# Two tiles for the fold of the row maxima, one mask instead of two, and norm weights in shared tiles, in a hybrid attention block on one core

## The chip, the cores and the metric

One core of a Trainium2 chip runs the whole kernel. The metric is the device time of one execution in microseconds, lower is better; a kernel's time is the median of its runs. Engines are named as in the profile: PE is TensorE (PEld its weight loads), DVE is VectorE, ACT is ScalarE, POOL is GpSimd, SP is the sync engine that issues most DMAs.

## What is computed

One decoder layer over 2048 tokens of width 1024: RMSNorm, one input projection, three mixers side by side (latent attention with 8 heads, differential attention with 4 heads of two softmax maps, cross-attention of 4 heads to 256 memory tokens), a SiLU gate and an output projection on top of the residual.

```
h = rms_norm(x, norm_g)
cq, ckv, kr, dq, dk, dv, mq, z = split(h @ w_in)
y_mla  = mla_branch(cq, ckv, kr, positions, ...)
y_diff = diff_branch(dq, dk, dv, positions, ...)
y_mem  = mem_branch(mq, mem, ...)
y = concat(y_mla, y_diff, y_mem) * silu(z)
x = x + y @ w_out
...
# in a causal branch, per block of queries:
sc = where(causal_mask, (q @ k.T) * scale, -1e30)
p  = softmax(sc)
```

## The kernel before

The work is cut into steps: 4 steps m (memory attention), 8 steps d (differential attention, 2 groups of 2 heads), 16 steps a (latent attention, 4 groups of 2 heads); in each group b = 0 to 3 counts blocks of 512 queries. Values are kept as a 16-bit part and a low remainder, so most products are three matmuls (L187 to L189 the projections, L917 to L919 the scores of a step a, L958 to L960 the output).

Softmax needs a bound on each query's row of scores. The kernel estimates it ahead: est_block (L387 to L421) multiplies the 16-bit parts of queries and keys (L398), adds the causal mask on the diagonal by a second matmul into the same PSUM tile (L400), and takes the maximum. For b = 0 VectorE takes it straight from PSUM (L402). For b of 1 to 3 (`fold`) ScalarE copies the first 512 keys of two query tiles into the halves of a tile er (L404), copies each later 512 into a tile ec (L407), VectorE takes the maximum into er (L408), folds er three times (L412) and reduces the last 64 columns (L413):

```
394  er = wk.tile([P, 2, 512], BF16, tag="er", name="er", bufs=1)
404  A.activation(er[:, t % 2], ps, AF.Copy)
408  V.tensor_tensor(er[:, t % 2, 0:n], er[:, t % 2, 0:n], ec[:, 0:n], ALU.max)
412  V.tensor_tensor(er[:, :, 0:n], er[:, :, 0:n], er[:, :, n:2 * n], ALU.max)
413  V.reduce_max(mx[:, m, t - 1:t + 1, 0], er[:, :, 0:64], axis=AX.X)
```

The estimate goes into a column of the query tile (L421), which is transposed again by a DMA on SP (L474 and L484 in a step d, L891 and then L900 in a step a) into a tile qB. Only then can the scores of that head start: L572 in a step d, L917 in a step a. The mask on the diagonal of the scores is a matmul with a second mask tile (mask_t, L575 and L921). ScalarE takes the exponential (L506), VectorE its low remainder (L507), TensorE multiplies by the values (L516, L518, L536).

Pools and names that the change touches: er has one tile and ec four; PSUM has three tiles for estimates (ps_e), two for scores, two for projections. In pool sm, ss (sums of squares, L440 and L624) and rstd (L92, inverse roots, by GpSimd at L97 and L101) have two tiles each. rtab is one tile for the rope tables of a step (L328, GpSimd L332 to L335). The norm weights g_mk and g_mq (L208 to L210, used once, at L242), g_q, g_k and g_n (L304 to L307) have tiles of their own; lamw (L312) is a scratch tile for the lambda.

The order of the work: a planner of costs and due times (steps, fills, Task) only sets the order in which code is recorded and its priorities. From these a scheduler then lays out every engine's instructions once, before the run, by what it believes durations and buffers to be. On the chip each engine goes through its list in that order and waits at semaphores.

Of the kernel before, what the change touches and what calls it, by code (L numbers as in the profile page):

```python
# [11 lines left out]
F32 = mybir.dt.float32  # L12
F16 = mybir.dt.float16
BF16 = mybir.dt.bfloat16
I32 = mybir.dt.int32
AF = mybir.ActivationFunctionType
ALU = mybir.AluOpType
AX = mybir.AxisListType

P = 128  # L20
# [6 lines left out]
NEG = -1.0e30  # L27
# [13 lines left out]
def hybrid_block(ctx: ExitStack, tc: tile.TileContext, x, mem, positions, norm_g, w_in, mla_q_norm_g,  # L41
                 mla_kv_norm_g, w_uq, w_ukv, mla_qn_g, mla_kn_g, diff_qn_g, diff_kn_g, diff_lambda,
                 diff_subln_g, mem_norm_g, w_mem_kv, mem_qn_g, mem_kn_g, w_out, out):
    nc = tc.nc
# [20 lines left out]
    ident = cst.tile([P, P], BF16, name="ident")  # L65
    make_identity(nc, ident)
    mask_t = cst.tile([P, P], BF16, name="mask_t")
    make_lower_triangular(nc, mask_t, val=NEG, diag=False)
    mask_e = cst.tile([P, P], BF16, name="mask_e")
    make_causal_mask(nc, mask_e, mask_val=NEG)  # L70
    mhalf = cst.tile([P, 1], F32, name="mhalf")
# [11 lines left out]
    def gain_row(src, n, name):  # L83
        t = cst.tile([P, n], F32, name=name)
        SP.dma_start(t, src.broadcast_to([P, n]))
        return t
# [4 lines left out]
    def rstd_of(ss, shape, name, tag="rstd", eps=EPS):  # L91
        r = sm.tile([P, 32 if tag == "rstd" else 8], F32, tag=tag, name=name)  # L92
        n = int(np.prod(shape))
        rv = r[:, 0:n]
        if len(shape) == 2:
            rv = rv.rearrange("p (a b) -> p a b", b=shape[1])
        G.tensor_scalar(rv, ss, eps, None, ALU.add)  # L97
        m = mhalf
        if len(shape) == 2:
            m = m.unsqueeze(2)  # L100
        G.tensor_tensor(rv, rv, m.broadcast_to([P] + list(shape)), ALU.pow)  # L101
        return rv
# [99 lines left out]
    def tmp4(name):  # L202
        return wk.tile([P, 1024], F32, tag="t4", name=name, bufs=2)
# [3 lines left out]
    tc.cur_priority = top + 1000  # L207
    g_mk = gain_row(mem_kn_g, 64, "g_mk")  # L208
    g_mq = gain_row(mem_qn_g, 64, "g_mq")
    V.tensor_tensor(g_mk, g_mk, g_mq, ALU.mult)  # L210
    mk = []
# [91 lines left out]
    g_dk = gain_row(diff_kn_g, 32, "g_dk")  # L303
    g_q = gain_row(mla_qn_g, 96, "g_q")  # L304
    g_k = gain_row(mla_kn_g, 96, "g_k")
    g_n = cst.tile([P, 64], F32, name="g_n")
    V.tensor_tensor(g_n, g_q[:, 0:64], g_k[:, 0:64], ALU.mult)  # L307
    g_wo = cst.tile([P, 1], F32, name="g_wo")
    for i in range(2):
        SP.dma_start(g_wo[64 * i:64 * i + 64, :], diff_subln_g[0].rearrange("(p o) -> p o", o=1))  # L310
    V.tensor_scalar_mul(g_wo, g_wo, (1.0 - LAM_INIT) * WS)
    lamw = tmp4("lamw")  # L312
    lamt = lamw[:, 0:128].rearrange("p (a b) -> p a b", b=32)
    SP.dma_start(lamt.rearrange("p a b -> p (a b)"), diff_lambda.rearrange("o a b -> o (a b)").broadcast_to([P, 128]))
# [72 lines left out]
    def est_block(st, i, nmap, mcol, lhs, rhs):  # L387
# [3 lines left out]
        for m in range(nmap):  # L391
            for t in range(4):
                if fold and t % 2 == 0:
                    er = wk.tile([P, 2, 512], BF16, tag="er", name="er", bufs=1)
                for c in range(b + 1):
# [3 lines left out]
                    if c == b:  # L399
                        T.matmul(ps[:, t * P:n], lhsT=ident, rhs=mask_e, start=False, stop=True)  # L400
                    if not fold:
# [22 lines left out]
    def prep_d(st, units):  # L424
# [14 lines left out]
        yield 1.0  # L439
        ss = sm.tile([P, 32], F32, tag="ss", name=f"ss_{nm}")  # L440
        V.reduce_sum(ss, sq.rearrange("p (a d) -> p a d", d=32), axis=AX.X)
# [167 lines left out]
    def prep_m(st, units):  # L609
# [13 lines left out]
        yield 1.0  # L623
        ss = sm.tile([P, 32], F32, tag="ss", name=f"ss_{nm}")  # L624
        V.reduce_sum(ss[:, 0:16], sq.rearrange("p t (m d) -> p (t m) d", d=64), axis=AX.X)
# [93 lines left out]
    def kv_latents():  # L719
        units = []  # L720
        yield from load_w(w_in, [(256, 160)], gx, "lk", units)
        for b in range(NB):
# [11 lines left out]
            r = rstd_of(ss, [4], f"rlk{b}", "rstd_l")  # L734
            tb = rope_tabs(b, g_k[:, 64:96], f"kr{b}")
            kr = cst.tile([P, 4, 32], F32, name=f"krot{b}")
# [87 lines left out]
    def prep_a(st):  # L824
        g, b, nm = st.g, st.b, st.name
        tb = rope_tabs(b, g_q[:, 64:96], nm)
        q = new_qkv(f"qkv_{nm}")[:, :, 0:192].rearrange("p t (h d) -> p t h d", d=96)
# [436 lines left out]
```

## Time and profile before

| | |
|---|---|
| time, median of 3 runs | 1371.22 us (1367.65 to 1371.38) |
| the profiled execution's own time | 1372.15 us |
| its span, first to last instruction | 1370.3 us |
| mean granted TensorE clock | 0.989 |
| PE, DVE, ACT, POOL busy | 94%, 82%, 66%, 24% of the span |

A row of a group of instructions gives the source line, the engine, the operation, out<-in with shapes, the count, then busy time in us and the mean of one in ns, then the time the engine stood idle just before them and what ended it. Durations come from the profiled execution. A busy PE is counted by modelled ends of pipelined matmuls, so its idle time is a lower bound.

### The profile page before, as it was taken

How to read it: one execution, taken by the hardware profiler on the slowest of the kernel's cores; microseconds unless marked ns; L12 is line 12 of the kernel's file. 1: busy time of each engine (PE TensorE's matmuls, PEld its weight loads, DVE VectorE, ACT ScalarE, POOL GpSimd, SP SyncE). 2: the span in 40 equal slices, each digit the busy share in tenths (PEclk: the TensorE clock that was granted, in tenths of full speed). 3: DMA queues.
4: the chain of work that ended last, by engine and by line, in shares of the span. 5: the costliest groups of instructions: out<-in, count | busy, mean ns of one | idle time of the engine just before them, and what ended most of it. 6: DMA issues, size and time to landing. Idle time of an engine off the chain costs nothing.

```text
span 1370.3 us, 35041 instructions
## 1 busy us (share of the span) xinstructions
PE 1293.0 (94%) x13616; PEld 829.5 (61%) x13616; DVE 1123.1 (82%) x2713; ACT 903.9 (66%) x2163; POOL 333.9 (24%) x477
## 2 busy tenths in 40 slices
PE   5988999999999999999998999999999998999998
PEld 2434556667667767667775656666655665655554
DVE  4657888879889867889899889999998998886745
ACT  6656544677878646786896667677766877665521
POOL 2322232403042133113202143223243323200000
PEclk9999999999999999999999999999999999999999
DMA  7998844223113322447446166347525643275452
GB/s 231 199 208 184 184 111 101 59 60 88 41 25 71 79 34 60 78 110 193 124 98 144 40 167 150 84 107 167 109 71 118 145 99 55 40 155 158 141 184 70
DMA packets 294262, 155.52 MB, mean 113 GB/s; under 512 B 239952, under 2 KB 272848, under 8 KB 294096
## 3 DMA queue, kind: packets, MB, share of 16 engines
q1 hardware_dynamic: 294064, 153.29, 47.7%
q8 instruction: 106, 1.74, 0.5%
q14 instruction: 60, 0.49, 0.1%
q0 software_dynamic: 32, 0.00, 0.0%
HBM read 61.75 MB, written 34.34 MB: 70 GB/s over the span
## 4 chain that ended last, share of the span: by engine, by line
PE 56%; DVE 13%; POOL 9%; ACT 8%; DMA 8%; issue 4%; SPq 1%; ACTq 0%; DVEq 0%; POOLq 0%
PE pp L189 6%; PE pp L187 6%; PE pp L188 6%; PE pe L398 5%; DVE plo L507 4%; PE pv L518 3%; PE pv L516 3%; PE pv L536 3%; PE st L572 3%; PE pp L958 3%; PE pp L959 3%; PE pp L960 3%; PE st L917 3%; PE st L918 2%; PE st L919 2%
## 5 line engine op out<-in xcount | busy, mean ns | idle before, releaser
L506 ACT ACTIVATE p<-st 128x512 f32<-128x512 f32 (+3 forms) x672 | 356.2, 551 | 167.2 <-PE st L919 65.8
L507 DVE TENSOR_TENSOR plo<-p 128x512 f16<-128x512 f32 (+3 forms) x672 | 404.6, 615 | 63.1 <-ACT p L506 59.2
L407 ACT ACTIVATE ec<-pe 128x512 bf16<-128x512 f32 (+3 forms) x384 | 197.2, 536 | 39.2 <-PE pe L400 17.1
L516 PEld LDWEIGHTS <-p 128*128 128x128 bf16 x2304 | 186.0, 99 | 51.5 <-DVE y_a L924 4.7
L518 PEld LDWEIGHTS <-p 128*128 128x128 bf16 x2304 | 173.1, 98 | 39.4 <-issue 4.1
L408 DVE TENSOR_TENSOR er<-er,ec 128x512 bf16<-128x512 bf16 (+3 forms) x384 | 141.5, 378 | 29.9 <-ACT ec L407 15.2
L404 ACT ACTIVATE er<-pe 128x512 bf16<-128x512 f32 x192 | 110.0, 606 | 47.2 <-DVE mx_a L413 18.1
L536 PEld LDWEIGHTS <-plo 128*128 128x128 f16 x2304 | 123.1, 97 | 23.7 <-DVE plo L507 5.8
L917 PE MATMUL st<-qB_a,kT_a 97*128 97x512 f16 (+1 forms) x320 | 112.8, 353 | 13.6 <-ACT p L506 8.7
L516 PE MATMUL pv<-V_d,p 128*128 128x65 f16 x1088 | 116.8, 194 | 3.3 <-DVE y_d L579 2.9
L189 PEld LDWEIGHTS <-ht_x 128*128 128x128 f16 x896 | 87.7, 98 | 52.9 <-ACT ht_x L137 3.9
L188 PEld LDWEIGHTS <-ht_x 128*128 128x128 f16 x896 | 87.8, 98 | 47.8 <-issue 4.0
L518 PE MATMUL pv<-V_d,p 128*128 128x64 f16 x1088 | 116.5, 196 | 0.0
L572 PE MATMUL st<-qB_d,kT_d 97*128 97x512 f16 (+1 forms) x320 | 111.4, 353 | 5.2 <-ACT zc L704 2.1
L187 PEld LDWEIGHTS <-ht_x 128*128 128x128 f16 x896 | 87.7, 98 | 47.1 <-issue 2.8
L516 PE MATMUL pv<-V_a,p 128*128 128x65 f16 x1088 | 112.6, 193 | 2.0 <-DVE y_a L924 1.9
L918 PE MATMUL st<-qB_a,kT_a 96*128 96x512 f16 (+1 forms) x320 | 112.6, 352 | 0.0
L398 PE MATMUL pe<-kT_d,qB_d 96*128 96x512 f16 (+2 forms) x320 | 106.2, 348 | 6.8 <-ACT ec L407 3.6
L518 PE MATMUL pv<-V_a,p 128*128 128x64 f16 x1088 | 112.2, 195 | 0.0
L919 PE MATMUL st<-qB_a,kT_a 96*128 96x512 f16 (+1 forms) x320 | 111.9, 350 | 0.0
L398 PE MATMUL pe<-kT_a,qB_a 96*128 96x512 f16 (+2 forms) x320 | 100.0, 349 | 7.7 <-DMA qB_a<-qs_a 4.6
L189 PE MATMUL pp<-w_d,ht_x 128*128 128x512 f16 x256 | 97.0, 379 | 0.0
(293 smaller groups left out, 3337.7 us busy)
## 6 DMA issues: line engine op xcount, KB each, us to landing
xt_x<-in_x_dram SPq DMA_DIRECT2D x16, 512.0 KB, 4.7
xr<-in_x_dram SPq DMA_DIRECT2D x16, 512.0 KB, 3.6
part<-xr SPq DMA_DIRECT2D x16, 512.0 KB, 2.9
ysc<-yt SPq DMA_DIRECT2D x31, 256.0 KB, 2.3
yl<-ysc SPq DMA_DIRECT2D x15, 512.0 KB, 4.6
zsc<-zc SPq DMA_DIRECT2D x48, 128.0 KB, 2.1
xa<-part SPq DMA_DIRECT2D x12, 512.0 KB, 3.6
out_dram<-xa SPq DMA_DIRECT2D x12, 512.0 KB, 2.9
```

The source lines that it names most:

```text
L187: T.matmul(ps[:, :n], lhsT=ht[:, 0, k], rhs=wt[:, 0, :n], start=(k == 0), stop=False)
L188: T.matmul(ps[:, :n], lhsT=ht[:, 0, k], rhs=wt[:, 1, :n], start=False, stop=False)
L189: T.matmul(ps[:, :n], lhsT=ht[:, 1, k], rhs=wt[:, 0, :n], start=False, stop=(k == NK - 1))
L398: T.matmul(ps[:, 0:n], lhsT=lhs(m, t), rhs=rhs(m, c, n // P), start=True, stop=c < b)
L407: A.activation(ec[:, 0:n], ps[:, 0:n], AF.Copy)
L506: A.activation(p32[:, :n], ps[:, :n], AF.Exp, scale=self.scale)
L507: V.tensor_tensor(plo[:, :n], p32[:, :n], phi[:, :n], ALU.subtract)
L516: T.matmul(pvv[:, t, 0:65], lhsT=phi[:, c], rhs=vt[:, 0:65], start=(j == 0 and t == 0), stop=False, skip_group_check=True)
L518: T.matmul(pvv[:, t, 0:64], lhsT=phi[:, c], rhs=vt[:, 65:129], start=False, stop=False, skip_group_check=True)
L536: last["pv"] = T.matmul(pvv[:, t, 0:65], lhsT=plo[:, c], rhs=vt[:, 0:65], start=False, stop=(j == self.njt - 1), skip_group_check=True)
L572: T.matmul(ps[:, :n], lhsT=st.kTs[j // 4][0:97, h, j % 4, m % 2, :], rhs=st.qB[h][0:97, t0:4, m % 2, :], start=True, stop=not diag)
L917: T.matmul(ps[:, :n], lhsT=kt[0:97, h, j % 4, 0, :], rhs=q[0:97, 0, t0:4, :], start=True, stop=False)
```

## The change

The fold gets two er tiles. To make room, the mask of the estimates, mask_e, goes away: the matmul that added it as ident^T times mask_e now takes mask_t as the stationary operand and ident as the moving one, which is mask_t transposed. The tiles ss and rstd get one buffer. g_mk and g_mq become the halves of a tile under the tag rtab. g_q and g_k shrink to the 32 rope columns; g_n is loaded by itself and multiplied by weights that are loaded into lamw. That makes two small DMAs on SP more and two set-up instructions on GpSimd fewer; all other engines have as many instructions as before.

```diff
-    mask_e = cst.tile([P, P], BF16, name="mask_e")
-    make_causal_mask(nc, mask_e, mask_val=NEG)
...
-        r = sm.tile([P, 32 if tag == "rstd" else 8], F32, tag=tag, name=name)
+        r = sm.tile([P, 32 if tag == "rstd" else 8], F32, tag=tag, name=name, bufs=1 if tag == "rstd" else 2)
...
-    g_mk = gain_row(mem_kn_g, 64, "g_mk")
-    g_mq = gain_row(mem_qn_g, 64, "g_mq")
-    V.tensor_tensor(g_mk, g_mk, g_mq, ALU.mult)
+    g_m2 = wk.tile([P, 2, 64], F32, tag="rtab", name="g_m2", bufs=1)
+    SP.dma_start(g_m2[:, 0], mem_kn_g.broadcast_to([P, 64]))
+    SP.dma_start(g_m2[:, 1], mem_qn_g.broadcast_to([P, 64]))
+    g_mk = g_m2[:, 0]
+    V.tensor_tensor(g_mk, g_mk, g_m2[:, 1], ALU.mult)
...
-    g_q = gain_row(mla_qn_g, 96, "g_q")
-    g_k = gain_row(mla_kn_g, 96, "g_k")
-    g_n = cst.tile([P, 64], F32, name="g_n")
-    V.tensor_tensor(g_n, g_q[:, 0:64], g_k[:, 0:64], ALU.mult)
+    g_q = gain_row(mla_qn_g[:, 64:96], 32, "g_q")
+    g_k = gain_row(mla_kn_g[:, 64:96], 32, "g_k")
+    g_n = gain_row(mla_qn_g[:, 0:64], 64, "g_n")
...
+    SP.dma_start(lamw[:, 192:256], mla_kn_g[:, 0:64].broadcast_to([P, 64]))
+    V.tensor_tensor(g_n, g_n, lamw[:, 192:256], ALU.mult)
...
-                    er = wk.tile([P, 2, 512], BF16, tag="er", name="er", bufs=1)
+                    er = wk.tile([P, 2, 512], BF16, tag="er", name="er", bufs=2)
...
-                        T.matmul(ps[:, t * P:n], lhsT=ident, rhs=mask_e, start=False, stop=True)
+                        T.matmul(ps[:, t * P:n], lhsT=mask_t, rhs=ident, start=False, stop=True)
...
-        ss = sm.tile([P, 32], F32, tag="ss", name=f"ss_{nm}")
+        ss = sm.tile([P, 32], F32, tag="ss", name=f"ss_{nm}", bufs=1)
```

The scheduler lays out all engines anew. Three places show how. In the rows, numbers tell tiles of one name apart; numbers of the change are lower by 4 for the same tile, and source lines move by 1 or 2 (L404 of before is L405 of the change, L917 is L918, L196 is L194).

VectorE, in the first estimate of a step d with b = 1. Before:

```order
L408 TENSOR_TENSOR er_2542<-er_2542,ec_2558 128x256
L583 SCALAR_TENSOR_TENSOR y_d00_2868<-pv_3110,rl_3164,y_d00_2868 128x64 x4
L412 TENSOR_TENSOR er_2542<-er_2542 128x2x256
L412 TENSOR_TENSOR er_2542<-er_2542 128x2x128
L412 TENSOR_TENSOR er_2542<-er_2542 128x2x64
L413 TENSOR_REDUCE mx0_d01_2541<-er_2542 128x2
L507 TENSOR_TENSOR plo_3177<-p32_3176 128x256
L507 TENSOR_TENSOR plo_3206<-p32_3205 128x128
L705 SCALAR_TENSOR_TENSOR zc002_3019<-zc002_3019,pp_2994 128x256
L408 TENSOR_TENSOR er_2565<-er_2565,ec_2598 128x384
```

After the change:

```order
L409 TENSOR_TENSOR er_2538<-er_2538,ec_2554 128x256
L584 SCALAR_TENSOR_TENSOR y_d00_2864<-pv_3106,rl_3160,y_d00_2864 128x64 x4
L413 TENSOR_TENSOR er_2538<-er_2538 128x2x256
L409 TENSOR_TENSOR er_2561<-er_2561,ec_2594 128x384
L413 TENSOR_TENSOR er_2538<-er_2538 128x2x128
L413 TENSOR_TENSOR er_2538<-er_2538 128x2x64
L414 TENSOR_REDUCE mx0_d01_2537<-er_2538 128x2
```

The first maximum into the second tile moved from behind the reduction of the first tile to between its folds.

ScalarE, in the estimate of step d03 (er_5238 before, er_5234 after, the same tile). Before:

```order
L196 ACTIVATE kl0_6589<-pp_6704 128x160
L726 ACTIVATE lsk0_6750<-kl0_6589 128x4x128
L727 ACTIVATE lsk0_6750<-kl0_6589 128x4x32
L506 ACTIVATE p32_6085<-st_6083 128x512
L404 ACTIVATE er_5238<-pe_5239 128x512
L404 ACTIVATE er_5238<-pe_5306 128x512
L407 ACTIVATE ec_5331<-pe_5329 128x512
```

After the change:

```order
L408 ACTIVATE ec_5227<-pe_5224 128x256
L405 ACTIVATE er_5234<-pe_5235 128x512
L434 ACTIVATE qkv_d10_5805<-pp_6256 128x256
L370 ACTIVATE V_d10_5806<-pp_6256 128x2x64
L507 ACTIVATE p32_5676<-st_5674 128x512
L439 ACTIVATE sq_d10_6395<-qkv_d10_5805 128x1024
L408 ACTIVATE ec_5257<-pe_5255 128x512
L375 ACTIVATE zt_d10_5807<-pp_6256 128x128
L507 ACTIVATE p32_5725<-st_5723 128x512
L408 ACTIVATE ec_5262<-pe_5260 128x512
```

The first copy into that tile moved ahead of the last projection of step d10 (qkv_d10, V_d10, sq_d10) and of all of the latents (kl0, lsk0), which it used to follow.

TensorE, in the estimates of head 1 of step a31 (qB1_a31), from the first of its eight L398 on. Before:

```order
L398 MATMUL pe_21267<-kT_a30_20656,qB1_a31_21194 128x512
L917 LDWEIGHTS kT_a21_18622
L917 MATMUL st_20961<-qB1_a23_19747,kT_a21_18622 128x512
L918 LDWEIGHTS kT_a21_18622
L918 MATMUL st_20961<-qB1_a23_19747,kT_a21_18622 128x512
```

After the change:

```order
L399 MATMUL pe_21263<-kT_a30_20652,qB1_a31_21190 128x512
L399 LDWEIGHTS qB1_a31_21190
L399 MATMUL pe_21266<-kT_a31_21149,qB1_a31_21190 128x128
L401 LDWEIGHTS mask_t_89
L401 MATMUL pe_21266<-ident_84,mask_t_89 128x128
L399 LDWEIGHTS qB1_a31_21190
L399 MATMUL pe_21272<-kT_a30_20652,qB1_a31_21190 128x512
L537 LDWEIGHTS plo_20802
```

The first estimate was followed by scores of another head, and the second stood 130 rows further; now the first three follow each other, and the eight lie within 60 rows instead of 448.

## Rows read from the trace of the kernel before

**Rows 1.** The page, busy us, share of the span and instructions of each engine.

```profile
PE 1293.0 (94%) x13616; PEld 829.5 (61%) x13616; DVE 1123.1 (82%) x2713; ACT 903.9 (66%) x2163; POOL 333.9 (24%) x477
```

**Rows 2.** Windows: stretch, its us, busy PE, PEld, DVE, ACT, POOL, clock, DMA.

```profile
200.00:1000.00 800.00, 775.94 (x8879) 534.66 (x8877) 696.07 (x1790) 572.18 (x1462) 209.04 (x275) 0.99 0.41 95
1000.00:1200.00 200.00, 182.69 (x2163) 119.53 (x2162) 182.47 (x439) 144.10 (x351) 70.86 (x91) 0.97 0.41 88
411.90:415.30 3.40, 2.96 (x46) 2.57 (x46) 3.35 (x12) 3.40 (x15) 0.56 (x2) 0.50 0.09 18
...
1176.50:1183.30 6.80, 6.37 (x29) 2.74 (x29) 5.43 (x10) 3.26 (x7) 6.52 (x8) 0.50 0.32 61
```

**Rows 3.** Waits of PE: waiter <- waited for: us in total, times, longest.

```profile
PE st L917 <- ACT p L506: 8.7, 13, 2.5
...
PE pe L398 <- ACT ec L407: 4.5, 8, 1.5
PE st L917 <- DMA qB_a<-qs_a: 4.3, 4, 1.5
...
PE pe L398 <- ACT er L404: 3.5, 6, 1.4
```

**Rows 4.** Waits of ACT.

```profile
ACT er L404 <- DVE mx_a L413: 18.1, 16, 3.7
...
ACT er L404 <- DVE mx_d L413: 15.1, 15, 3.1
...
ACT ec L407 <- DVE er L408: 7.0, 7, 2.6
```

**Rows 5.** Groups of instructions by line, ACT.

```profile
L407 ACT ACTIVATE ec<-pe 128x512 bf16<-128x512 f32 (+3 forms) x384 | 197.2, 536 | 39.2 <-PE pe L400 17.1 <-PE pe L398 10.9 <-DVE er L408 7.0
...
L404 ACT ACTIVATE er<-pe 128x512 bf16<-128x512 f32 x192 | 110.0, 606 | 47.2 <-DVE mx_a L413 18.1 <-DVE mx_d L413 15.1 <-PE pe L398 11.4
```

**Rows 6.** Timeline around 409 us (start, us, engine, instruction, idle before).

```profile
408.69 1.09 ACT L404 ACTIVATE er<-pe 128x512 bf16<-128x512 f32 x2 [3.15 <-DVE mx_d L413]
...
408.38 0.27 DVE L413 TENSOR_REDUCE mx_d<-er 128x2 f32<-128x128 bf16 x1
...
409.33 0.38 PE L398 MATMUL pe<-kT_d,qB_d 96*128 96x512 f16 x1 [1.43 <-ACT er L404]
```

**Rows 7.** Timeline of PE, the four scores that waited for a transpose.

```profile
1130.27 0.38 PE L917 MATMUL st<-qB_a,kT_a 97*128 97x512 f16 x1 [1.31 <-DMA qB_a<-qs_a]
...
1153.39 0.38 PE L917 MATMUL st<-qB_a,kT_a 97*128 97x512 f16 x1 [0.48 <-DMA qB_a<-qs_a]
...
1176.93 0.58 PE L917 MATMUL st<-qB_a,kT_a 97*128 97x512 f16 x1 [1.10 <-DMA qB_a<-qs_a]
...
1214.03 0.39 PE L917 MATMUL st<-qB_a,kT_a 97*128 97x512 f16 x1 [1.45 <-DMA qB_a<-qs_a]
```

**Rows 8.** Timeline of the start: SP, then ACT, then PE.

```profile
15.10 0.33 SPq L85 DMA_DIRECT2D g_q<-in_mla_qn_g_dram  x1
16.40 0.33 SPq L85 DMA_DIRECT2D g_k<-in_mla_kn_g_dram  x1
...
21.70 0.43 SPq L120 DMA_DIRECT2D xt_x<-in_x_dram  x1
...
27.22 1.06 ACT L143 ACTIVATE xh_x<-xt_x 128x1024 f16<-128x1024 f32 x1 [0.57 <-DMA xt_x<-in_x_dram]
...
32.49 0.38 PE L134 MATMUL pt<-ident,xl_x 128*128 128x128 bf16 x4 [2.65 <-DVE ht_x L137]
```

**Rows 9.** Lines L242 and L332 (count, ns, first and last start), and timeline of r_d.

```profile
L242 DVE TENSOR_TENSOR mem_kn<-mem_kn,g_mk x1: 684/684/684, 67.6 to 67.6; 128x512 f32<-128x512 f32 x1
...
L332 POOL TENSOR_TENSOR rt_d<-cos_t,g_dk x8: 318/404/4525, 127.0 to 546.6; 128x64 f32<-128x64 f32 x8
...
269.36 0.68 DVE L457 TENSOR_TENSOR qkv_d<-qkv_d,r_d 128x512 f32<-128x512 f32 x1
...
314.98 0.30 POOL L97 TENSOR_SCALAR r_d<-ss_d 128x32 f32<-128x32 f32 x1 [29.90 <-DVE ss_d L441]
```

More of the change, by code (lines that the diff above doesn't have):

```diff
@@ L8 @@
 from concourse import mybir
-from concourse.masks import make_causal_mask, make_identity, make_lower_triangular
+from concourse.masks import make_identity, make_lower_triangular
 from concourse._compat import with_exitstack
@@ L623, in prep_m @@
         yield 1.0
-        ss = sm.tile([P, 32], F32, tag="ss", name=f"ss_{nm}")
+        ss = sm.tile([P, 32], F32, tag="ss", name=f"ss_{nm}", bufs=1)
         V.reduce_sum(ss[:, 0:16], sq.rearrange("p t (m d) -> p (t m) d", d=64), axis=AX.X)
@@ L734, in kv_latents @@
             r = rstd_of(ss, [4], f"rlk{b}", "rstd_l")
-            tb = rope_tabs(b, g_k[:, 64:96], f"kr{b}")
+            tb = rope_tabs(b, g_k, f"kr{b}")
             kr = cst.tile([P, 4, 32], F32, name=f"krot{b}")
@@ L825, in prep_a @@
         g, b, nm = st.g, st.b, st.name
-        tb = rope_tabs(b, g_q[:, 64:96], nm)
+        tb = rope_tabs(b, g_q, nm)
         q = new_qkv(f"qkv_{nm}")[:, :, 0:192].rearrange("p t (h d) -> p t h d", d=96)
```

## The prediction, made before the changed kernel was run

> **What bounds the kernel now.** I read the busy shares first, then stretches, then the waits of TensorE and ScalarE, then the instructions around the longest of these waits. In the busy shares TensorE stands at 94%, VectorE at 82%, ScalarE at 66% [rows 1]. The stretches show that this is no even mix: from 200 to 1000 us TensorE is idle for 24 us of 800, but from 1000 to 1200 us for 17 of 200, and there VectorE is busy for as long as TensorE, 182.5 against 182.7 us [rows 2]. All matmuls stay, so what can be won is TensorE's idle time, 1370.3 - 1293.0 = 77 us, and what a lowered clock costs after it.
>
> Who ends that idle time is in the waits of TensorE [rows 3]. The scores wait for an exponential (8.7 us) or for a transposed query tile (4.3 us); the estimate of the row maxima (L398) waits for ScalarE to empty a PSUM buffer into er (3.5 us) or ec (4.5 us). ScalarE, for its part, stood still before its copies into er until the last VectorE instruction of the fold before, L413: 18.1 + 15.1 = 33.2 us in 31 waits [rows 4]. That is the single er tile: the 192 copies (606 ns each) fill 96 tiles [rows 5], and each new tile needs the old one folded. The longest of these cases shows the mechanism: VectorE gets to L413 at 408.38, ScalarE had been idle for 3.15 us when it starts er at 408.69, and TensorE, idle for 1.43 us, starts the next estimate at 409.33 [rows 6]. Directly after, from 411.9 to 415.3, the granted clock is 0.50, the lower of its two levels (1.2 and 2.4 GHz); the same stands from 1176.5 to 1183.3 [rows 2].
>
> **The change part by part.**
>
> *Second er tile, direct part.* The copy into er now waits for the fold two tiles back. TensorE's 3.5 us behind er should go. Of the 4.5 us behind ec I take half, 2.2, since such an ec follows an er in ScalarE's queue. Term: -5.7 us; bounds 0 (VectorE is late in any case, and ec, four tiles, stops ScalarE next) and -8.0 (both rows). That the other 25 of the 33.2 us were worth anything I don't assume: TensorE had other matmuls.
>
> *Estimates that stand earlier.* The compiler laid all engines out anew. The four waits of scores for the second transpose of their query tile (1.31, 0.48, 1.10 and 1.45 us, together 4.3) [rows 7] belong, counted along the order, to head 1 of step a22, both heads of a23 and head 1 of a31. Between the last estimate and the first scores of that head stood 354, 212, 294 and 370 rows of TensorE's order; now 516, 588, 668 and 848. The transpose itself is as long as it was, but it starts that much sooner. Term: -4.3 us; bounds 0 (the transposes queue on SP behind others) and -4.3.
>
> *The clock.* Half of TensorE's busy time at the lower level is lost: in 411.9 to 415.3 it is 2.96 / 2, in 1176.5 to 1183.3 it is 6.37 / 2 [rows 2], together 4.7 us. The first follows an er wait [rows 6], the second the transpose wait that ends at 1176.93 [rows 7]. Term: -4.7 us; bounds 0 and -4.7.
>
> *Packing.* This is what the new order costs. The eight estimate matmuls of head 1 of a31 stood within 448 rows of TensorE's order and now stand within 60. Each must be emptied by ScalarE (536 to 606 ns [rows 5]) and folded by VectorE, and TensorE has three PSUM buffers to run ahead with; what it is stopped at, everything behind it is stopped at too. No row shows this. The nearest one is the wait of ec for VectorE's maximum, 7.0 us in 7 cases [rows 4]: it is what ScalarE loses where VectorE can't keep up, and with denser estimates more of it reaches TensorE. Bounds: 0 (other matmuls lie between) and +12 (below, second rival). I take the row, +7.0 us.
>
> *Start.* The weights now take two more loads on SP ahead of the fourth row tile of x, since g_n, g_q and g_k load their own parts and the other half of g_n's product comes through lamw. Loads of this kind follow each other at 15.10 and 16.40; the tile of x is issued at 21.70, ScalarE waits for it until 27.22, and in VectorE's order the copies that TensorE's wait of 2.65 us ends with (32.49) stand behind that tile's low part [rows 8]. Two issues of 0.33 us are the least, two spacings of 1.30 the most: +0.7 to +2.6; ScalarE's slack is spent, so I take +1.5.
>
> *What costs nothing.* The mask matmul keeps shape and count; only which of two 128x128 tiles is loaded and which one streams changes. Two set-up instructions leave GpSimd before anything waits for it. g_m2 in the tile of the rope tables is read for the last time at 67.6 and first written by a table at 127.0 [rows 9]: 59 us of cover, without which GpSimd would wait. One tile each for ss and rstd: r_d of one step is read for the last time at 269.36, and the next step writes it at 314.98 [rows 9]; the cover is the distance between steps, and if it were gone, each of the 28 preparations (4 m, 8 d, 16 a) could stop GpSimd.
>
> **The sum** against the profiled execution (1372.15 us): -5.7 - 4.3 - 4.7 + 7.0 + 1.5 = -6.2, so 1366.0. That execution stands 0.93 us above the median of the runs (1371.22), so 1365.0 on the median's scale. A measurement of this kernel can tell about 0.3%, 4.1 us, from no change: below 1367.1 is faster, above 1375.3 slower.
>
> **The rivals.**
>
> *VectorE sets the pace: no change, 1371.* For it: between 1000 and 1200 us it is as busy as TensorE [rows 2], and the er waits end with VectorE's fold, which runs no faster. A second tile then only moves ScalarE's wait from er to ec and to the exponentials. Against it: VectorE is idle for 18% of the whole span [rows 1]. The terms from er and the clock then shrink to about -1.5, the transposes' stays, packing takes it back: -1.5 - 4.3 + 4.0 + 1.5, about 1371. The Trainium skill, Perfetto Trace Analysis, section Identifying the Most-Contended Engine, would have one work on the engine of highest occupancy and judge TensorE by its weight loads instead of its matmuls. By that rule VectorE (82%) comes before TensorE (weight loads 61%), and a change that takes no instruction off VectorE brings nothing. The rows agree in part, between 1000 and 1200 us alone.
>
> *Packed estimates stop TensorE: slower, 1379.* The place is L398 in the d and a steps, 36 blocks with a fold (12 in d, 24 in a). One wait for ec cost TensorE 4.5 / 8 = 0.56 us [rows 3]. If one such wait comes per block, that is 20 us where 8.0 stood: +12. Without term one: 1372.15 + 12 - 4.3 - 4.7 + 1.5 = 1376.7; two more stretches at the lower clock (2.96 / 2 each) make it 1379.6, or 1379 on the median's scale. It decides from the point at which waits of L398 for er and ec together grow by more than the 7.5 us that transposes, clock and start bring. For it: the order is made with no knowledge of the chip's delays, and VectorE has little to spare late in the span. Against it: until 1000 us TensorE is nearly never starved with the same estimates, and the second er lets VectorE lag by one more tile.
>
> *The exponentials profit too: 1355.* ScalarE's 33.2 us of standing still are in one queue with the exponentials. If half of the 8.7 us of scores that wait for them [rows 3] goes with two more stretches at the lower clock (3.0 us) and packing costs only 4: -5.7 - 4.3 - 4.7 - 4.4 - 3.0 + 4.0 + 1.5 = -16.6, or 1355. Against it: around most of those waits ScalarE was busy with projections and stacks, not waiting for er.
>
> That the change doesn't do what it says can be left out: VectorE's order shows a maximum of the next tile ahead of the last folds of the one before.
>
> **How the numbers follow.** Forecast (1365, own range 1358 to 1369) 0.45; no change 0.23; slower 0.20; larger gain 0.12. Of the forecast's 0.45 about 0.07 lies above 1367.1. Faster: 0.38 + 0.12 = 0.50. Same: 0.07 + 0.21 = 0.28. Slower: 0.20 + 0.02 = 0.22. The range goes from 1353, below which some 0.05 of the larger gain lies, to 1380, above which lies half of the slower case.
>
> **What would show it.** Right: the waits of er for L413 fall from 33 us to under 10; L917 no longer waits for qB_a at the four places; no lowered clock near 412 and 1177; TensorE idle for some 76 us (77 - 5.7 - 4.3 + 7.0 + 1.5). Packing at its price: L398's waits for ec and er together are 8 to 10 us, mostly ec. Wrong: those waits at 16 or more (slower), er's wait replaced by one of equal size for ec (no change), or new gaps of TensorE that no step here names, since the whole order was laid out anew.

## The result and the profile after

The changed kernel takes 1379.46 us (median of 5 runs, 1376.52 to 1382.19), the kernel before beside it 1371.34 (5 runs, 1367.65 to 1373.46): a ratio of 1.0054, with a 95% interval of 1.0031 to 1.0077. It is slower by 0.5%, where the forecast was 1365, a gain. The profiled execution takes 1379.46 us, with a span of 1377.7 against 1370.3. Lines after L70 stand a few lines off: L398 is now L399, L404 L405, L407 L408, L413 L414, L506 L507, L917 L918; in the kernels of the experiments they are a few lines off again (L396 to L404 for L398).

The page's busy times of the changed kernel, to be read beside [rows 1]:

```profile
PE 1295.7 (94%) x13616; PEld 830.6 (60%) x13616; DVE 1109.4 (81%) x2713; ACT 901.3 (65%) x2163; POOL 346.8 (25%) x475
```

TensorE is busy for 2.7 us more with the same instructions and idle for 82.0 instead of 77.3 us (the prediction had 76). Who ends its idle time, first two rows of the kernel before that [rows 3] leaves out:

```profile
PE pe L398 <- DMA qB_a<-qs_a: 4.6, 3, 2.0
...
PE pe L398 <- DMA qB_d<-s_d: 0.5, 1, 0.5
```

then the changed kernel:

```profile
PE st L918 <- ACT p L507: 12.8, 17, 2.5
PE pe L399 <- DMA qB_a<-qs_a: 9.4, 5, 3.1
...
PE pt L132 <- DVE ht_x L135: 4.6, 1, 4.6
...
PE pe L399 <- ACT er L405: 3.6, 3, 2.1
...
PE pe L399 <- ACT ec L408: 3.2, 7, 0.8
PE pe L399 <- DMA qB_d<-s_d: 2.5, 2, 1.8
```

and ScalarE's before er:

```profile
ACT er L405 <- DVE mx_d L414: 4.9, 3, 2.7
...
ACT er L405 <- DVE mx_a L414: 3.1, 4, 1.7
```

What the change was to do, it did: er waits for the fold for 8.0 instead of 33.2 us [rows 4], and the row of scores waiting for qB_a [rows 3, 7] is gone. But the estimates' waits for er and ec fell only from 8.0 to 6.8 us, the scores' waits for an exponential rose from 8.7 to 12.8, and two rows have grown that no step of the prediction names: the estimates wait longer for the *first* transpose of their own query tile, 9.4 us in the a steps (5 cases, 4.6 in 3 before) and 2.5 in the d steps (0.5 before). The two longest on TensorE's timeline:

```profile
747.00 0.72 PE L399 MATMUL pe<-kT_a,qB_a 96*128 96x512 f16 x2 [2.54 <-DMA qB_a<-qs_a]
...
807.26 0.66 PE L399 MATMUL pe<-kT_a,qB_a 96*128 96x512 f16 x3 [3.12 <-DMA qB_a<-qs_a]
```

One trace of each would not be enough for this, since a wait differs from trace to trace. But all three kernels with the changed order (the changed one, and after_no_loads and gn_on_gpsimd below) lie outside the six that have the order of before, but for a few places (the kernel before, and mask_only, sums_single, norms_before_order, two_loads and two_er_before_order below):

| TensorE's waits, us | order of before | changed order |
|---|---|---|
| scores of a steps for an exponential | 6.4 to 8.7 | 11.8 to 12.8 |
| estimates for the first transpose, a steps | 2.7 to 5.7 | 9.4 to 11.7 |
| estimates for the first transpose, d steps | 0.5 to 2.2 | 2.5 to 3.6 |
| estimates for er and ec | 8.0 to 11.2 | 6.6 to 7.1 |

The start lost more than the two issues on SP. On the timelines of VectorE, ScalarE, SP and TensorE:

```profile
26.63 0.23 DVE L313 TENSOR_TENSOR g_n<-g_n,lamw 128x64 f32<-128x64 f32 x1 [1.77 <-DMA lamw<-in_mla_kn_g_dram]
...
28.78 0.20 ACT L321 ACTIVATE lams<-lams 128x2 f32<-128x2 f32 x1 [2.75 <-DVE lams L320]
29.75 1.06 ACT L141 ACTIVATE xh_x<-xt_x 128x1024 f16<-128x1024 f32 x1 [0.77 <-DMA xt_x<-in_x_dram]
...
22.82 0.43 SPq L118 DMA_DIRECT2D xt_x<-in_x_dram  x1
...
35.02 0.58 PE L132 MATMUL pt<-ident,xl_x 128*128 128x128 bf16 x4 [4.62 <-DVE ht_x L135]
```

SP issues the fourth tile of x 1.1 us later than before [rows 8], but ScalarE takes it up 2.5 us later, and what it waits for last is this tile's own transfer (0.77 us): from the issue to ScalarE's start are 6.9 us, where it was 5.5 (21.70 to 27.22). In the traces of the experiments (but for the two with a late set-up) that tile takes 5.3 to 6.7 us to land without the two further loads and 6.9 to 7.4 with them; what makes it longer isn't shown. The exponential of lambda (L321), which stands ahead of it and waits for VectorE and its late small weights, is done at 28.98 and so isn't what sets this start. TensorE resumes 2.5 us later, at the lower clock for longer; the first scores of step m00 start 3.3 us later (78.3 against 75.0), those of m01 4.6 later. The clock, as stretches of the changed kernel (columns as in [rows 2]):

```profile
33.00:39.80 6.80, 4.79 (x21) 2.55 (x21) 5.36 (x7) 6.80 (x14) 0.84 (x2) 0.50 0.49 142
101.30:108.10 6.80, 5.77 (x17) 2.54 (x17) 4.92 (x11) 4.29 (x9) 1.31 (x3) 0.50 0.98 175
125.20:132.00 6.80, 5.76 (x14) 2.08 (x14) 3.38 (x9) 5.75 (x10) 1.91 (x6) 0.50 0.32 75
418.80:422.20 3.40, 2.94 (x49) 2.67 (x49) 3.40 (x11) 3.40 (x13) 2.18 (x4) 0.51 0.01 5
746.40:753.20 6.80, 6.20 (x20) 2.53 (x21) 0.39 (x2) 1.25 (x3) 0.00 (x0) 0.50 0.72 195
777.20:780.60 3.40, 3.40 (x55) 2.89 (x52) 1.51 (x3) 1.83 (x4) 0.12 (x1) 0.51 0.02 5
807.90:811.30 3.40, 3.40 (x11) 1.17 (x9) 1.02 (x3) 2.29 (x12) 0.94 (x2) 0.50 0.20 44
1152.60:1156.00 3.40, 3.40 (x10) 1.19 (x9) 3.40 (x15) 1.85 (x4) 0.00 (x0) 0.50 0.09 18
1176.50:1183.30 6.80, 6.56 (x89) 4.15 (x89) 6.80 (x14) 5.08 (x10) 6.47 (x6) 1.00 0.44 87
```

The first eight rows are all its stretches at the lower level, 40.8 us, where the trace of the kernel before has 30.6 us in 7. Of the two stretches that the prediction named, the one near 1177 is gone (last row). The one near 412 is not: it stands at 418.8, at the same place of the work (in both kernels TensorE has then done 102 of the 320 score products of the d steps), and again right behind a wait for er:

```profile
417.76 0.38 PE L399 MATMUL pe<-kT_d,qB_d 96*128 96x512 f16 x1 [2.13 <-ACT er L405]
```

Three other stretches begin in one of the waits shown above, or right after it: the waits that end at 35.02, 747.00 and 807.26. How much of the 10 us is the change's can't be told from two traces: kernels with the order of before have from 24 us in 7 stretches (sums_single) to 44 in 11 (mask_only). The mean granted clock of all runs tells more. It is 0.9850 for the five runs of the changed kernel and 0.9874 (from 0.982 to 0.993) for the 100 runs of the kernel before beside the experiments. The time at the lower level is twice what is missing to 1, times the span: an estimated 41 and 35 us. Half of that is lost, so the changed kernel loses some 3 us more, uncertain by as much.

### The profile page after: what moved, and what is told of

Its sections match the earlier page's. It is cut to its first block, busy times and chain, and to the rows that moved or that the text cites. A ratio compares the mean times of both kernels' runs of the same rounds, so it can differ in the third digit from the quotient of the medians.

```text
span 1377.7 us, 35144 instructions
## 1 busy us (share of the span) xinstructions
PE 1295.7 (94%) x13616; PEld 830.6 (60%) x13616; DVE 1109.4 (81%) x2713; ACT 901.3 (65%) x2163; POOL 346.8 (25%) x475
## 4 chain that ended last, share of the span: by engine, by line
PE 55%; DVE 15%; DMA 11%; POOL 8%; ACT 7%; issue 4%; SPq 1%; ACTq 0%; DVEq 0%; POOLq 0%
PE pp L185 6%; PE pp L187 6%; PE pp L186 6%; PE pe L399 5%; DVE plo L508 5%; PE pp L959 3%; PE pp L960 3%; PE pp L961 3%; PE pv L519 3%; PE pv L537 3%; PE pv L517 3%; DMA qB_a<-qs_a 3%; PE st L573 2%; PE st L918 2%; PE st L919 2%
## 5 line engine op out<-in xcount | busy, mean ns | idle before, releaser
L507 ACT ACTIVATE p<-st 128x512 f32<-128x512 f32 (+3 forms) x672 | 358.2, 554 | 186.6 <-PE st L920 72.8
L408 ACT ACTIVATE ec<-pe 128x512 bf16<-128x512 f32 (+3 forms) x384 | 199.4, 546 | 39.6 <-PE pe L399 18.2
L405 ACT ACTIVATE er<-pe 128x512 bf16<-128x512 f32 x192 | 118.0, 621 | 26.4 <-PE pe L399 17.7
L918 PE MATMUL st<-qB_a,kT_a 97*128 97x512 f16 (+1 forms) x320 | 111.4, 348 | 13.2 <-ACT p L507 12.8
L399 PE MATMUL pe<-kT_d,qB_d 96*128 96x512 f16 (+2 forms) x320 | 105.7, 348 | 7.9 <-ACT er L405 3.6
L919 PE MATMUL st<-qB_a,kT_a 96*128 96x512 f16 (+1 forms) x320 | 111.1, 347 | 0.0
L920 PE MATMUL st<-qB_a,kT_a 96*128 96x512 f16 (+1 forms) x320 | 110.4, 345 | 0.0
L399 PE MATMUL pe<-kT_a,qB_a 96*128 96x512 f16 (+2 forms) x320 | 93.8, 350 | 13.2 <-DMA qB_a<-qs_a 9.4
```

Source lines behind the costliest of these rows:

```text
L399: T.matmul(ps[:, 0:n], lhsT=lhs(m, t), rhs=rhs(m, c, n // P), start=True, stop=c < b)
L408: A.activation(ec[:, 0:n], ps[:, 0:n], AF.Copy)
L507: A.activation(p32[:, :n], ps[:, :n], AF.Exp, scale=self.scale)
L918: T.matmul(ps[:, :n], lhsT=kt[0:97, h, j % 4, 0, :], rhs=q[0:97, 0, t0:4, :], start=True, stop=False)
```

## Experiments

All ratios are to runs of the kernel before on the same chip; brackets are 95% intervals.

### First question: the start, or the second tile?

**one_er**: the changed kernel with one er tile.

```diff
-                    er = wk.tile([P, 2, 512], BF16, tag="er", name="er", bufs=2)
+                    er = wk.tile([P, 2, 512], BF16, tag="er", name="er", bufs=1)
```

> The change with one er tile again; the mask, the shared and trimmed norm weights, ss and rstd stay changed. Theory A (the start: two more small loads and their sums hold VectorE and ScalarE in order until the fourth row tile is late, and the lower clock lasts one stretch longer): the first scores of step m00 are late by 3 to 5 us against before, the rest runs as before, total 1375 to 1377. Theory B (the estimates that the second er tile lets the scheduler pull ahead run into other waits): the loss goes with the tile, total 1371, first scores of m00 no more than 1 us late. The forecast's rival (packed estimates stop TensorE at er and ec): also 1371.

1397.62 us, 1.0189 [1.0163, 1.0215]. No theory had that. The start's delay is there (first scores of m00 3.6 us late), but the other 22 us come between the last d steps and a23. So without the second tile the "free" edits cost 26 us: something in them holds the kernel back, or something else changes with them.

**late_setup** and **before_late_setup**: the set-up of g_q, g_k, g_n, g_wo and lambda is recorded later, ahead of the rope tables, in the changed kernel and in the kernel before.

```diff
-    g_q = gain_row(mla_qn_g[:, 64:96], 32, "g_q")
...
+    def late_tables():
...
     def d_feed():
+        late_tables()
         rope_tables()
```

> The change, with the loads and sums of g_q, g_k, g_n, g_wo and the lambda recorded later, just ahead of the rope tables, so that VectorE and ScalarE no longer meet them in the first 30 us. Theory A: the first scores of m00 come at 75 us or sooner instead of 78, total 1379.5 - 4.6 = 1375 or less; what is then left against before is the price of the second er tile's order, some +3. Theory B: total stays above 1377.

> The kernel before with the same set-up moved later. Theory A: before loses at the start too (VectorE 2.1 us and ScalarE 0.8 us behind lamw), so the first scores of m00 come 1 to 3 us sooner and the total is 1368 to 1371. Theory B says nothing: 1371.

1392.72 us, 1.0148 [1.0123, 1.0173], and 1385.49, 1.0103 [1.0078, 1.0127]. The first scores of m00 came 1.6 and 1.0 us later than in the kernel before, not sooner as theory A had it, and both are far slower than what they were made from. In before_late_setup the loss comes hundreds of us after the edit (the first scores of a01 are still 0.7 us early); late_setup is 10.8 us late at m02 already, 2.6 at d01, and loses again later.

### Second question: which of the free edits?

**mask_only**: the kernel before with the transposed mask and no mask_e.

```diff
-    make_causal_mask(nc, mask_e, mask_val=NEG)
...
-                        T.matmul(ps[:, t * P:n], lhsT=ident, rhs=mask_e, start=False, stop=True)
+                        T.matmul(ps[:, t * P:n], lhsT=mask_t, rhs=ident, start=False, stop=True)
```

> The kernel before with the one mask used transposed, nothing else. Every theory: the matmul costs the same (220 ns), total 1371 within 0.3%. If it moves by more, the layout that the scheduler makes of a change that costs nothing is itself worth some us, and smaller differences of the other runs can't be put down to an edit.

1372.84 us, 1.0001 [0.9986, 1.0015]: nothing.

**sums_single**: the kernel before with one tile each for ss and rstd.

```diff
-        r = sm.tile([P, 32 if tag == "rstd" else 8], F32, tag=tag, name=name)
+        r = sm.tile([P, 32 if tag == "rstd" else 8], F32, tag=tag, name=name, bufs=1 if tag == "rstd" else 2)
-        ss = sm.tile([P, 32], F32, tag="ss", name=f"ss_{nm}")
+        ss = sm.tile([P, 32], F32, tag="ss", name=f"ss_{nm}", bufs=1)
```

> The kernel before with one tile each for ss and rstd, and nothing else of the change. Theory C (the single small tiles are what the second er tile has to pay for; they hold back the preparations of d and a steps): 1385 to 1395 us, nothing lost at the start (first scores of m00 within 1 us of before), the loss builds up from the last d steps on, as it did with one er tile, and ScalarE's ks_a waits longer for GpSimd's kn_a (13.2 us before). Theory D (the norm weights and the start are the cost): 1370 to 1375, no difference from before.

1370.80 us, 0.9992 [0.9977, 1.0007]: nothing; theory C falls.

**norms_only**: the kernel before with the change's norm weights, the lines of the diff above from g_m2 to g_n, g_q and g_k.

> The kernel before with the shared and trimmed norm weights (g_m2 in the rope tables' tile, g_q and g_k trimmed, g_n's product through lamw), and nothing else. Theory C: only the start's price, 3 to 5 us, so 1374 to 1377, with the first scores of m00 3 us later and nothing further lost. Theory D: the late start grows along the span, as it did when the set-up was moved: 1380 to 1392.

1398.59 us, 1.0179 [1.0159, 1.02]: the whole loss of one_er, so theory D by its number. The two kernels also have the same order on TensorE, ScalarE and VectorE. But weights that are read a few times for each step should hardly cost 25.7 us (the third question puts this to the test), and the first scores of d11 are only 6.3 us late: the rest again comes from d12 on.

**two_er_three_ec**: the kernel before with two er tiles, three ec tiles, the transposed mask and g_m2.

```diff
-                    er = wk.tile([P, 2, 512], BF16, tag="er", name="er", bufs=1)
+                    er = wk.tile([P, 2, 512], BF16, tag="er", name="er", bufs=2)
-                        ec = wk.tile([P, 512], BF16, tag="ec", name="ec", bufs=4)
+                        ec = wk.tile([P, 512], BF16, tag="ec", name="ec", bufs=3)
```

> The kernel before with two er tiles, the transposed mask and g_m2 in the rope tables' tile; the room comes from a fourth ec tile (three stay). ss, rstd and the other norm weights are as before. Theory C, and theory D alike: the second er tile without its price, 1353 to 1362; the first scores of m00 within 1 us of before. If a third ec tile is needed as much as the second er tile: 1371 or more, with ScalarE's waits before ec (L407) for VectorE's maximum well above 7.0 us.

1393.40 us, 1.0141 [1.0121, 1.0162]. No trimmed weights, no late start, and still 19 us lost. ScalarE's waits at ec for VectorE are 7.8 us, not well above 7.0.

**gn_on_gpsimd**: the changed kernel with g_n's product on GpSimd.

```diff
-    V.tensor_tensor(g_n, g_n, lamw[:, 192:256], ALU.mult)
+    G.tensor_tensor(g_n, g_n, lamw[:, 192:256], ALU.mult)
```

> The changed kernel with the product of g_n on GpSimd, so that VectorE doesn't wait for the load through lamw in its order. If VectorE's stand at that product is what makes the start late: first scores of m00 1 to 2 us later than before (in the changed kernel 3.3), a lowered clock near 33 us for 3.4 instead of 6.8 us, and 1374 to 1377 in all. If the two further loads on SP are: m00 stays 3 us late, and 1378 to 1381.

1377.79 us, 1.0037 [1.0021, 1.0053], m00 3.3 us late as before. VectorE's stand at this one product (26.63 above) is not what sets the start. In this kernel VectorE's next waits, for the loads of lambda and of two more weights, last until 28.73, and the exponential of lambda starts at 29.04, so the loads themselves are left.

### Third question: the edits or the order?

The scheduler had laid out ScalarE and VectorE anew in each of the kernels that lost 13 us or more, one_er among them; mask_only and sums_single have the orders of the kernel before there, instruction by instruction. So the same trimmed weights were set up in two ways, of which one leaves the order as it was.

**norms_before_order** (GpSimd copies; orders of TensorE, ScalarE and VectorE as in the kernel before) and **norms_new_order** (VectorE copies; orders of TensorE and ScalarE as in norms_only):

```diff
-    g_q = gain_row(mla_qn_g, 96, "g_q")
-    g_k = gain_row(mla_kn_g, 96, "g_k")
+    lamw = tmp4("lamw")
+    SP.dma_start(lamw[:, 192:288], mla_qn_g.broadcast_to([P, 96]))
+    SP.dma_start(lamw[:, 288:384], mla_kn_g.broadcast_to([P, 96]))
     g_n = cst.tile([P, 64], F32, name="g_n")
-    V.tensor_tensor(g_n, g_q[:, 0:64], g_k[:, 0:64], ALU.mult)
+    V.tensor_tensor(g_n, lamw[:, 192:256], lamw[:, 288:352], ALU.mult)
+    g_q = cst.tile([P, 32], F32, name="g_q")
+    g_k = cst.tile([P, 32], F32, name="g_k")
+    G.tensor_copy(g_q, lamw[:, 256:288])
+    G.tensor_copy(g_k, lamw[:, 352:384])
...
-    lamw = tmp4("lamw")
```

(norms_new_order has V in the last two lines. Both have g_m2 as in the change.)

> The kernel before with g_q and g_k trimmed, g_n by itself and g_m2 in the rope tables' tile, as in norms_only, but set up differently: both full rows are loaded once into lamw, GpSimd copies the rope columns. No load is added, and the compiler leaves the orders of TensorE, ScalarE and VectorE as they are in the kernel before. Theory O (norms_only lost its 25.7 us by the new order that the scheduler laid out, not by the trimmed tiles): 1370 to 1376, first scores of m00 within 1.5 us, no loss between d12 and a01. Theory N (the trimmed and shared tiles themselves hold the engines back): 1390 or more, with the loss at d12 to a01 as in norms_only.

> As norms_before_order, but VectorE copies the rope columns, and with that the scheduler lays out TensorE's and ScalarE's order exactly as in norms_only, without its two more loads on SP. Theory O: 1391 to 1398, the same loss of some 10 us at d12 and of more at a00 to a13 as norms_only. Theory N: the same time as norms_before_order.

1373.97 us, 1.0004 [0.9988, 1.0021], and 1393.70, 1.0156 [1.0132, 1.018]. Two copies of 32 columns on another engine make 20 us, and what differs with them is the order of everything after. The trimmed tiles cost nothing. ScalarE's waits tell the two orders apart; first norms_before_order:

```profile
ACT ks_a L884 <- POOL kn_a L873: 12.6, 10, 3.0
ACT s_d L471 <- DVE qkv_d L463: 11.6, 9, 4.6
...
ACT qs_a L891 <- DMA kT_a<-ks_a: 8.5, 5, 3.2
```

then norms_new_order:

```profile
ACT ks_a L884 <- POOL kn_a L873: 22.6, 13, 4.1
...
ACT s_d L471 <- DVE qkv_d L463: 20.2, 10, 5.2
...
ACT qs_a L891 <- DMA kT_a<-ks_a: 18.4, 11, 2.6
```

These are the copies that build the stacked key and query tiles of a later step. In the worse order they stand in ScalarE's queue at places where their input, or a free stack tile, comes later, and behind them stands what TensorE needs, as in this one case on norms_new_order's timeline (SP, ScalarE, TensorE):

```profile
1197.86 1.40 SPq L888 DMA_TRANSPOSE kT_a<-ks_a  x1
...
1201.85 0.52 ACT L891 ACTIVATE qs_a<-qkv_a 128x384 f16<-128x384 f32 x1 [2.08 <-DMA kT_a<-ks_a]
1202.28 0.47 ACT L413 ACTIVATE ec<-pe 128x384 bf16<-128x384 f32 x1
...
1202.80 0.58 PE L404 MATMUL pe<-kT_a,qB_a 96*128 96x512 f16 x1 [2.61 <-ACT ec L413]
```

ScalarE stands at qs_a until a transposing DMA has read a stack tile, ec is late by that, and TensorE by ec.

**two_loads**: the kernel before with two more loads on SP into unused columns; orders unchanged.

```diff
     lamw = tmp4("lamw")
+    SP.dma_start(lamw[:, 256:320], mla_qn_g[:, 0:64].broadcast_to([P, 64]))
+    SP.dma_start(lamw[:, 192:256], mla_kn_g[:, 0:64].broadcast_to([P, 64]))
```

> The kernel before with two more loads of 64 weights on SP into unused columns of lamw, ahead of lambda's; nothing else, and the orders of TensorE, ScalarE and VectorE stay. It measures the start term by itself. If these loads are the start's price: first scores of m00 2.5 to 4 us later, a longer lowered clock at 33 us, 1374 to 1377. If only what VectorE waits for counts: within 1 us of before, 1371 to 1374.

1373.47 us, 1.0001 [0.9984, 1.0017]. The start is late as expected (m00 by 2.5 us), but nothing of it shows in the time. Where it goes can't be read from the traces: two_loads is 4.2 us late at a22 and 1.6 at a30, but mask_only, which has no load more and the same order, is as late there (4.3 and 3.7).

**after_no_loads**: the changed kernel with the weights set up as in norms_new_order; its own orders of TensorE and ScalarE stay.

> The changed kernel with both full rows loaded once into lamw and the rope columns copied by VectorE: no load more than before, and the orders of TensorE and ScalarE as in the changed kernel. What is left is its order and the second er tile. If the start's 3 to 5 us stay to the end: 1373 to 1377; if they are swallowed by later waits: 1377 to 1381.

1373.57 us, 1.0007 [0.999, 1.0025], against 1.0054 for the changed kernel: here the same two loads cost 0.5%, some 6 us (some 4 by gn_on_gpsimd, which has them too), so the start's price stays to the end. m00 is 0.7 us late instead of 3.3, and by the mean clock of its twelve runs (0.9872) the lower level takes an estimated 35 us again instead of 41. Why the loads are paid in this order and not in that of the kernel before isn't shown. This kernel has the longer waits of the changed one (11.8 us for exponentials, 9.5 and 3.6 for first transposes) and yet takes no longer than the kernel before. So it isn't these waits that make the changed kernel the slower one: they take back no more than the order and the second tile gain, and the two loads make the difference.

### Fourth question: what is the second tile worth?

**two_er_before_order** and **two_er_own_order**: the changed kernel, weights set up as in norms_before_order. The first is held to the order of the kernel before: every instruction gets an edge to the one that stood ahead of it on its engine there, which orders them without a wait. The second has the scheduler's own order.

```diff
         hybrid_block(tc, *args)
+        keep_order(nc, tc)
...
+            tc.add_manual_dep(ins[int(b)], ins[int(a)].name, nosync, reason="order")
```

> The changed kernel, its weights set up as in norms_before_order (no load more than before), and every engine held to the order of the kernel before by explicit order edges. The only thing left of the change that can matter is the second er tile. Theory E (the second tile is worth something where the order stays): ScalarE's er waits for L413 fall from 33 us to under 12, TensorE's waits for er and ec from 8.0 us to 2 to 6, 1362 to 1369. Theory F (the waits of ScalarE that it removes were covered; er waits for VectorE become ec waits, since VectorE sets the pace there): 1369 to 1375 with er's waits gone and TensorE's waits for ec as long or longer.

> The same kernel without the order edges: the scheduler's own order for two er tiles when the start is as in the kernel before. Up to d12 that order is the changed kernel's, after that it is like the one of two_er_three_ec. Theory O (the order decides): 1386 to 1396, the loss from a02 on as in two_er_three_ec, though all four ec tiles are there. If in two_er_three_ec the missing ec tile was the cost: 1370 to 1378.

1371.61 us, 0.9985 [0.9974, 0.9996], and 1395.70, 1.0159 [1.0136, 1.0182]. The two kernels differ in nothing but the order. With the order of before held, the second tile alone brings 0.15%, 2.1 us. ScalarE's waits of er for the fold are gone from the list; what is left of its waits for VectorE, and TensorE's waits, in two_er_before_order:

```profile
ACT ec L411 <- DVE er L412: 10.3, 7, 4.5
```

```profile
PE pe L402 <- ACT ec L411: 7.0, 8, 3.3
...
PE pe L402 <- ACT er L408: 2.0, 3, 1.1
```

TensorE's wait for er falls from 3.5 to 2.0 us and that for ec rises from 4.5 to 7.0 [rows 3]: together 9.0, where the five kernels with this order and one er tile have 8.0 to 11.2. So no fall is shown. Of ScalarE's 33 us before er, 13 come back before the same copies: er now waits for TensorE's estimate (17.2 instead of 11.4 us), and ec for the estimate (31.7 instead of 28.0) and for VectorE (10.3 instead of 7.0 [rows 4]). That is what theory F expected. The case of [rows 6] shows it, first on TensorE in the kernel before, then in two_er_before_order on ScalarE, VectorE and TensorE, and last the clock there (columns as in [rows 2]):

```profile
411.68 0.43 PE L398 MATMUL pe<-kT_d,qB_d 96*128 96x512 f16 x1 [1.49 <-ACT ec L407]
```

```profile
407.00 1.08 ACT L408 ACTIVATE er<-pe 128x512 bf16<-128x512 f32 x2
412.58 0.60 ACT L411 ACTIVATE ec<-pe 128x512 bf16<-128x512 f32 x1 [4.50 <-DVE er L412]
...
411.99 0.56 DVE L412 TENSOR_TENSOR er<-er,ec 128x512 bf16<-128x512 bf16 x1
...
413.23 0.56 PE L402 MATMUL pe<-kT_d,qB_d 96*128 96x512 f16 x1 [3.27 <-ACT ec L411]
```

```profile
413.30:416.70 3.40, 3.09 (x46) 2.52 (x46) 3.36 (x12) 3.39 (x15) 0.49 (x1) 0.50 0.04 9
```

ScalarE copies into er without a wait, but then stands at ec until VectorE has come to its maximum. TensorE is idle for 3.27 us, where it was 1.43 for er and 1.49 for the next ec in the kernel before, and the lower clock follows as before.

The scheduler's own order for the same kernel costs 24 us more, with all four ec tiles, so in two_er_three_ec too the order can account for the loss without the missing ec tile.

### Fifth question: what in the worse order costs?

**stack_new_order** and **stack_before_order**: all other edits as in two_er_before_order, but one er tile; its 2 KB go into a seventh stack tile (ks and qs). In stack_new_order VectorE copies the rope columns, as in norms_new_order. Held to the order of norms_new_order and of the kernel before.

```diff
-        return wk.tile(shape, F16, tag="s2", name=name, bufs=6)
+        return wk.tile(shape, F16, tag="s2", name=name, bufs=7)
```

> norms_new_order, held to its own order (the 21 us worse one), with one er tile and a seventh stack tile. There ScalarE waits 18.4 us at qs_a for the DMA of ks_a. If that wait is what the new order costs (it stands ahead of the ec and p that TensorE's longest gaps end with): 1378 to 1388. If the cost lies in other waits of the same order (ks_a for GpSimd's kn_a 22.6 us, s_d 20.2 us, the clock): 1389 to 1396.

> As two_er_before_order, held to the order of the kernel before, but the 2 KB go into a seventh tile for the stacks (ks, qs of a step) instead of a second er tile. ScalarE's waits at qs_a for the transposing DMA of ks_a (8.8 us before) and at ks_a for that of qB_a (6.1) should go. If a wait of ScalarE is covered in this order whichever it is: 1370 to 1374, like two_er_before_order. If the stacks are what TensorE's waits for p (8.7 us) come from: 1364 to 1369.

1383.57 us, 1.0076 [1.005, 1.0101], and 1365.44, 0.995 [0.993, 0.997]. In the worse order the row of qs_a waiting for ks_a's DMA is gone, and half of that order's loss with it (1.0156 to 1.0076). Two other long waits stay, in stack_new_order (its trace is of its fastest run, 1377.47 us); whether they are the rest isn't shown:

```profile
ACT s_d L469 <- DVE qkv_d L461: 23.1, 12, 5.1
ACT ks_a L882 <- POOL kn_a L871: 22.6, 12, 4.1
```

In the good order the stack tile takes 0.5%, 6.9 us, off the kernel before: ScalarE's 8.8 us at qs_a for ks_a's DMA and 6.1 at ks_a for qB_a's are gone, and the scores' waits for an exponential fall to 5.1 us (8.7 in the kernel before, 6.4 to 8.1 in the others with this order), though er still waits for the fold as long as ever:

```profile
ACT er L408 <- DVE mx_a L417: 19.7, 17, 3.7
...
ACT er L408 <- DVE mx_d L417: 15.1, 15, 3.1
```

```profile
PE st L921 <- ACT p L510: 5.1, 9, 1.9
```

This is the fastest version, and it beats both kernels.

## Why the prediction was wrong

The sign was wrong. Three steps failed: the direct part of the second tile, the price of the new order, and the start. The measured +0.54% splits by ratios into three parts: the second tile alone -0.15%, the new order for it +0.22% (after_no_loads against two_er_before_order), the two loads in that order +0.47%, uncertain by 0.1, 0.2 and 0.3%. That is -2, +3 and +6 us, if the parts add up, and the middle one is barely clear of nothing. The prediction had -5.7 for the first, -4.3 - 4.7 + 7.0 = -2.0 for the second and +1.5 for the third. That the measured time still lies in its range, at the end that belonged to a rival, is chance.

- *Second er tile, direct part* (-5.7): wrong. Its mechanism came in half: ScalarE no longer waits for the fold, but TensorE's waits for er and ec together fell by 1.2 us in the changed kernel and show no fall with the order held. The step that failed is that the 3.5 us behind er "should go" and half of ec's with them; at the prediction's own example the wait passed on to ec (3.27 us), as the rival "VectorE sets the pace" said. (That example is the longest wait for er of the d steps; in the a steps one is 3.7 us [rows 4].) The Trainium skill, Perfetto Trace Analysis, section Identifying the Most-Contended Engine, says which engine to work on first; by it that is VectorE, 82% busy against 61% of weight loads. That a change which takes no instruction off VectorE brings nothing is the prediction's own conclusion from it, and the runs go against it: the second tile brings 2.1 us, and the seventh stack tile 6.9, with VectorE busy for 1123.5 us as before (1123.1 [rows 1]).
- *Estimates that stand earlier* (-4.3): right for the waits that it names, all four are gone. Wrong as a sum: in the new order the estimates wait longer for the first transpose of their own query tile. That wait went from 4.6 to 9.4 us in the a steps, and the d steps' from 0.5 to 2.5; the step counted distance to the second transpose only and passed over the row of 4.6 us.
- *The clock* (-4.7): wrong. The step tied each stretch to one wait. The one near 412 it put down to an er wait, but the last wait ahead of it was one of 1.49 us for ec, until 411.68, and the stretch came back at the same place of the work in the changed kernel and with the order held. The one near 1177 is gone, but two_er_before_order, in which all four transpose waits stand (4.3 us), has no lower clock between 1045 us and its last microsecond either. By the estimate from the runs' mean clock the changed kernel loses some 3 us more than the kernel before, not 4.7 less.
- *Packing* (+7.0): did not happen as described. L399's waits for er and ec are 6.8 us, under the 8 to 10 forecast and far from the 16 of "Packed estimates stop TensorE". That rival gave 1379 and met the time by luck, since another mechanism made it. Its mechanism is real elsewhere: in norms_new_order L404 waits 11.7 us for ec and 2.7 for er.
- *Start* (+1.5): too small. SP was late by the 1.1 us foreseen, but TensorE by 2.5 and the first scores by 3.3 to 4.6; the step counted the later issue of the tile of x and not that the tile would also take longer to come (6.9 instead of 5.5 us). In the end the two loads cost some 6 us, where the range was +0.7 to +2.6.
- *What costs nothing*: right for mask, ss, rstd, g_m2 and the trimmed weights as work (0.9992 to 1.0004). Wrong in what it left out: the same edits move the scheduler's order, and between the orders seen here lie 20 to 24 us, more than every term of the sum. The prediction priced the new order at a few places and took the rest of it for free.
- "Wrong: new gaps of TensorE that no step here names, since the whole order was laid out anew" is the sign that came true.

What is not settled: which feature of the order of two_er_own_order costs 24 us, why the changed kernel's order lies between, and why its order pays for the two loads.

## What to carry to other kernels

Where a scheduler lays out the engines from believed durations, a change in set-up code is also a new draw of the whole order: hold the order and change the buffers, or hold the buffers and change the order, before a gain or a loss is put down to either. A long wait of a helper engine is no measure of what its removal brings: 33 us before er were worth 2, some 15 us before the stack copies were worth 7, and the scores' waits for exponentials shrank with the second alone. So ask of each wait what stands behind it in the same queue, and who waits for that.

## What the runs showed that was not expected

- Two copies of 128x32 on VectorE instead of GpSimd, in the set-up, changed the time by 20 us through the order alone (norms_new_order against norms_before_order).
- A start that is 2.5 us late cost nothing measurable at the end in one order (1.0001, uncertain by 2 us) and some 6 us, uncertain by 4, in another.
- The stretches at the lower clock differ between traces with the same order of TensorE, ScalarE and VectorE and nearly the same time: 24 us in 7 stretches in sums_single (0.9992), 44 in 11 in mask_only (1.0001). One trace of each kernel can't price the clock.
